# The attention stage of a hybrid layer: one written order on four engines, the sink logit as a column of the scores, output-projection rows split earlier

## The chip, the cores and the metric

The kernel runs on one core of a Trainium2 chip. The metric is device time in microseconds of that core. It holds all tensors in float32; matrix products that need accuracy are made from float32r halves (a high part and the rest), three matmuls for one product.

## The reference, cut to what matters

The layer is a diffusion backbone block: a modulated RMS norm, one input projection whose columns feed an mLSTM head group and a windowed attention head group, one output projection over both, a gated residual, and a convolutional GLU mixer. The change touches the attention group and the output projection that is woven into it.

```python
# q: (1024, 8, 64) rotated and scaled; k, v: (1024, 2, 64); k_ctx, v_ctx: (256, 2, 64); sink: (8,)
s_band = einsum(q, k)                # three blocks of 128 keys around each block of 128 queries,
s_band = where(|i - j| <= 128, s_band, -inf)
s_ctx  = einsum(q, k_ctx)            # 256 context keys, no mask
s_sink = sink[head]                  # one learned logit for each head
p   = softmax(concat([s_band, s_ctx, s_sink], -1), -1)
y_a = p[band] @ v + p[ctx] @ v_ctx   # the sink has no value row
x   = x + g_a * (concat([y_m, y_a], -1) @ w_out)      # rows 0-511 of w_out serve the mLSTM half y_m
```

## The kernel before

The program is written in a tile framework. Inside a `manual_schedule` block the named engines run their instructions in the order in which they are written; everywhere else a planner with a cost table chooses the order on each engine. TensorE is PE, VectorE DVE, ScalarE ACT, GpSimd POOL; SP issues nearly all DMAs.

**Query projections.** `qgen` runs 16 projections (`qproj`, 24 matmuls of 128x256 each), rotates each (three DVE operations, `rotate`), splits and transposes it (`qtrans`) and stores it to DRAM (`q_d`). The first ones run woven into the last mLSTM head; when that head is done, the tiles of the attention stage are allocated, and each later projection also starts one piece of `kprep` (keys of one block of 128 tokens) and one entry of `loads`: two pieces of the value tile `vv`, then row block 0 of the output projection. `load_wo` loads 128 rows of `w_out` (a 128x1024 tile `wor`), multiplies them by the gate row `rga`, copies them to float32r (ACT) and subtracts (DVE) for the rest. In this stretch PE alone has a written order.

**Attention.** There are 32 pairs of heads: 8 query blocks times 4 pairs. Class `Pair` holds the steps: `S(j)` scores of one head into a two-bank PSUM tile `sps` (256 context columns and 256 or 384 band columns, then one or two mask matmuls), `mxo(j)` the negated maximum (DVE, and a second DVE operation that takes the minimum with the negated sink `nsink`), `ex(j)` the exponential with its sum (ACT), `nrm` (the sink's own exponential, its addition to the sum, the reciprocal, and two multiplications on POOL), `tr(i)` transposes of probabilities, two key blocks of two heads at a time, `hi(i)` and `lo(i)` their float32r halves (ACT and DVE), `pv(i)` the products with values into the PSUM tile `u`, and `y1`, `y2` which add the halves and store into `yTa`. Score tiles are single: one for each head of a pair. The loop of lines 1180 to 1234 writes step t with scores of pair t, normalisation of pair t-1 and products of pair t-2.

**Output projection in between.** `wout_m(b)` is the mLSTM half of the output projection for token block b: four transposes of `ym`, a split, then eight groups of three 128x512 matmuls into the single PSUM tile `po` (four groups for each half of the 1024 columns), with an addition of x and a store to `x2_d`. `wout_f(0)` is the attention half of block 0. These are generators; `slot()` advances them by a rate between the steps of the loop. Row blocks 1 to 3 of `w_out` are loaded after the projections (line 1166), row blocks 4 to 7 in blocks 4 to 6 (`WBS`). None of this stage is inside `manual_schedule`: the planner orders it on all engines.

**After the loop** the pools close, and a stage with a written order (line 1387) makes the attention half for the other blocks (`wout_n`), norms them and prepares the mixer.

Of the kernel before, what the change touches and what calls it, by code (L numbers as in the profile page):

```python
# [17 lines left out]
P = 128  # L18
# [20 lines left out]
RATE3 = 0.37  # L39
QB = 3  # L40
# [16 lines left out]
AHEAD = 4  # L57

# [15 lines left out]
def build(tc, I, out, dbg=None):  # L74
# [11 lines left out]
    nsink = cp.tile([P, AH], F32, name="nsink")  # L86
# [38 lines left out]
    hps = [p1.enter_context(tc.tile_pool(name=f"hp{n}", bufs=1)) for n in range(2)]  # L125
# [222 lines left out]
    with tc.manual_schedule(engines={mybir.EngineType.PE, mybir.EngineType.DVE, mybir.EngineType.Activation,  # L348
# [93 lines left out]
        V.tensor_scalar(out=nsink[:], in0=rwc("sink"), scalar1=-1.0, scalar2=None, op0=ALU.mult)  # L442
# [405 lines left out]
    def qproj(i, b):  # L848
        px = pd.tile([P, 512], F32, name="px", tag="d")
        for kt in range(KT):  # L850
            mm3(px[:, :256], hsl(0, kt, NC + b), hsl(1, kt, NC + b), wq[i][0][:, kt, :256], wq[i][1][:, kt, :256],
                kt == 0, kt == KT - 1)
            if kt % 2:
                yield 0.64
        if i == 0:
            zs.append(pq.tile([P, 2, 2 * P], F32, name="z", tag="p_", bufs=PB, padded_shape=[P, 2, 320]))
        rotate(zs[b][:, i], px[:, :256], 4, b)

    def qtrans(i, b):
# [9 lines left out]
        QT = pq.tile([P, 4, P], F32R, name="QTo", tag="QTo", bufs=2)  # L869
# [3 lines left out]
    def load_wo(kt, eng, pool, tag=None):  # L873
        raw = wm.tile([P, D], F32, name="wor", tag="wor", bufs=2)
        nc.sync.dma_start(raw[:], I["w_out"][kt * P:(kt + 1) * P, :])
        eng.tensor_tensor(out=raw[:], in0=raw[:], in1=rga[:], op=ALU.mult)
        hi, lo = (w4(F32R, "wo4") if tag else pool.tile([P, D], F32R, name=f"wo{n}{kt}") for n in "hl")
        S.copy(hi[:], raw[:])
        V.tensor_tensor(out=lo[:], in0=raw[:], in1=hi[:].bitcast(F32), op=ALU.subtract)
        return hi, lo  # L880
# [16 lines left out]
    zs, wos, kgens, loads = [], [], [], []  # L897
# [45 lines left out]
    for h in range(H):  # L943
# [20 lines left out]
        with tc.manual_schedule(engines=order_):  # L964
# [24 lines left out]
            if nh is None:  # L989
# [10 lines left out]
                loads += [lambda: load_vv(0), lambda: load_vv(1), lambda: wos.append(load_wo(0, V, wm))]  # L1000
# [18 lines left out]
    lw = lastk.enter_context(tc.tile_pool(name="lw", bufs=6))  # L1019
    w4 = lambda dt, n: lw.tile([P, D], dt, name=n, tag="w4")  # L1020
# [3 lines left out]
    def wout_m(b):  # L1024
        pt = pT.tile([P, 512], F32, name="pt", tag="l")
        for j in range(4):
            T.transpose(pt[:, j * P:(j + 1) * P], ym[:, b, j * P:(j + 1) * P], ident[:])
        yield
        ph = t2.tile([P, 512], F32R, name="ymh", tag="ymh", bufs=1)
        pl_ = t2.tile([P, 512], F32R, name="yml", tag="yml", bufs=1)  # L1030
        S.copy(ph[:], pt[:])
        yield
        V.tensor_tensor(out=pl_[:], in0=pt[:], in1=ph[:].bitcast(F32), op=ALU.subtract)
        xb = x2t()
        nc.sync.dma_start(xb[:], I["x"][b * P:(b + 1) * P, :])
        yield
        for n in range(2):
            ns = slice(512 * n, 512 * n + 512)
            po = pO.tile([P, 512], F32, name="po", tag="o")
            for kt in range(4):  # L1040
                js = slice(kt * P, (kt + 1) * P)
                mm3(po[:], ph[:, js], pl_[:, js], wos[kt][0][:, ns], wos[kt][1][:, ns], kt == 0, kt == 3)
                yield
            V.tensor_tensor(out=xb[:, ns], in0=po[:], in1=xb[:, ns], op=ALU.add)
            if n == 1:
                nc.sync.dma_start(x2_d[b][:], xb[:])
            yield

    def wout_f(b):
        bs = slice(b * P, (b + 1) * P)  # L1050
        yh = t2.tile([P, 4, P], F32R, name="yh", tag="ymh", bufs=1)
        yl = t2.tile([P, 4, P], F32R, name="yl", tag="yml", bufs=1)
        xb = t3.tile([P, D], F32, name="x2", tag="x2")
        xs[b] = xb[:]
        nc.sync.dma_start(xb[:], x2_d[b][:])
        S.copy(yh[:], yTa[:, :, bs])
        yield
        V.tensor_tensor(out=yl[:], in0=yTa[:, :, bs], in1=yh[:].bitcast(F32), op=ALU.subtract)
        yield
        for n in range(2):  # L1060
            ns = slice(512 * n, 512 * n + 512)
            po = pO.tile([P, 512], F32, name="po", tag="o")
            for kt in range(4):
                mm3(po[:], yh[:, kt], yl[:, kt], wos[4 + kt][0][:, ns], wos[4 + kt][1][:, ns], kt == 0, kt == 3)
                yield
            V.tensor_tensor(out=xb[:, ns], in0=po[:], in1=xb[:, ns], op=ALU.add)
            if n == 1:
                nc.sync.dma_start(x2_d[b][:], xb[:])
            yield

    class Pair:
        def __init__(self, b, g, r):
# [7 lines left out]
            self.p, self.sv, self.pt, self.ph, self.pl = [None] * 2, [None] * 2, [None] * 3, [None] * 3, [None] * 3  # L1080

        def S(self, j):
# [3 lines left out]
            sps = pSs[j][0].tile([P, 1024], F32, name="sps", tag=pSs[j][1])  # L1086
# [10 lines left out]
            self.sv[j] = sps[:, 256:256 + self.nk]  # L1097

        def mxo(self, j):
            V.tensor_reduce(out=self.nm[:, j:j + 1], in_=self.sv[j], axis=AX.X, op=ALU.max, negate=True)  # L1100
            V.tensor_tensor(out=self.nm[:, j:j + 1], in0=self.nm[:, j:j + 1], in1=nsink[:, self.h0 + j:self.h0 + j + 1],
                             op=ALU.min)

        def ex(self, j):
            self.p[j] = pq.tile([P, 640], F32, name="p_", tag="p_", bufs=PB)
            S.activation(self.p[j][:, :self.nk], self.sv[j], AF.Exp, bias=self.nm[:, j:j + 1], scale=1.0,
                         accum_out=self.ss[:, j:j + 1])
# [57 lines left out]

    wos += [load_wo(k, V, lw, "w4") for k in range(1, 4)]
    w0 = wout_m(0)
    next(w0)
    for g in qpend:
        next(g, 0)  # L1170
    for _ in w0:
        pass
    pdk.close()
    pSs = [(pk, "pp"), (pa_.enter_context(tc.tile_pool(name="pS", bufs=1, space=PSUM, side="right")), "s")]
    pairs = [(b, g, r) for b in range(NL) for g in range(KVH) for r in range(2)]
    live = {}
    fill = [wout_m(b) for b in range(1, NL)] + [wout_f(b) for b in range(NA)]
    rate = (13 * 7 + 12 * NA) / (8.0 * (len(pairs) + 2))
    null = type("N", (), {"__getattr__": lambda s, n: (lambda *a: None)})()
    for t in range(len(pairs) + 2):  # L1180
        blk, sub = divmod(t, 4)
        if sub == 0 and blk < NL:
            if blk + 1 < NL:
                lq = load_q(blk + 1)
            for kt in range(4, 8):
                if WBS[kt - 4] == blk:
                    with tc.issue_after(lq):
                        wos.append(load_wo(kt, G, wop))

        def slot(k=1.0):  # L1190
            global_debt[0] += rate * k
            while fill and global_debt[0] >= 1.0:
                global_debt[0] -= 1.0
                try:
                    next(fill[0])
                except StopIteration:
                    fill.pop(0)
        if t == 0:
            global_debt = [0.0]
        if t < len(pairs):  # L1200
            live[t] = Pair(*pairs[t])
        A = live.get(t, null)
        B = live.get(t - 1, null)
        C = live.get(t - 2, null)
        B.nrm()
        A.S(0)
        slot()
# [12 lines left out]
        C.lo(1)  # L1220
        C.pv(0)
        slot()
        A.ex(1)
        C.tr(2)
        C.hi(2)
        slot()
        C.lo(2)
        C.pv(1)
        slot()
        C.pv(2)  # L1230
        C.y1()
        slot()
        C.y2()
        live.pop(t - 2, None)
    for f_ in fill:
        for _ in f_:
            pass
# [8 lines left out]
    rst2 = ExitStack()  # L1246
    eW = top.enter_context(tc.tile_pool(name="eW", bufs=1, side="right", reuse_waits="tile"))
# [28 lines left out]
    def ysplit_h(b, eng=G):  # L1276
        ys[b] = [t3.tile([P, 4, P], F32R, name=f"y{n}", tag=f"y{n}", bufs=3 if n == "h" else 2) for n in "hl"]
# [769 lines left out]
```

## Time and profile before

| | |
|---|---|
| median of 3 runs | 1298.04 us (1297.0 to 1298.63) |
| the profiled execution | 1300.43 us |
| its span from first to last instruction | 1298.6 us |
| mean granted TensorE clock | 0.991 |
| busy in the span | PE 1255.1 us, DVE 993.2, ACT 630.7, POOL 208.1 |
| last matmul of the query projections starts | 402.12 us |
| first transpose of the stage after attention | 608.91 us |

Times in rows are microseconds from the span's start; a row of a timeline gives start, duration, engine, line, operation, output<-inputs, form and count, and in brackets the idle time of that engine before it and what ended it. PE's durations contain the drain of its pipeline, so successive starts and not durations tell what a matmul costs; the same holds, less strongly, for DVE and ACT.

### The profile page before, as it was taken

How to read it: one execution, taken by the hardware profiler on the slowest of the kernel's cores; microseconds unless marked ns; L12 is line 12 of the kernel's file. 1: busy time of each engine (PE TensorE's matmuls, PEld its weight loads, DVE VectorE, ACT ScalarE, POOL GpSimd, SP SyncE). 2: the span in 40 equal slices, each digit the busy share in tenths (PEclk: the TensorE clock that was granted, in tenths of full speed). 3: DMA queues.
4: the chain of work that ended last, by engine and by line, in shares of the span. 5: the costliest groups of instructions: out<-in, count | busy, mean ns of one | idle time of the engine just before them, and what ended most of it. 6: DMA issues, size and time to landing. Idle time of an engine off the chain costs nothing.

```text
span 1298.6 us, 19413 instructions
## 1 busy us (share of the span) xinstructions
PE 1255.1 (97%) x7071; PEld 1069.9 (82%) x7071; DVE 993.2 (76%) x1809; ACT 630.7 (49%) x1271; POOL 208.1 (16%) x171
## 2 busy tenths in 40 slices
PE   6999999999898999999989999999999999999997
PEld 4899998989897787888768888888888888788886
DVE  5763777867786789896898777777777776877887
ACT  6632555464864567676654333333333333434435
POOL 1200000000001223332412122222212222001000
PEclk9999999999998999999989999999999999999999
DMA  9431544352253313202423223332222336974653
GB/s 362 173 118 40 145 136 132 119 165 76 83 180 129 131 50 114 98 33 68 161 81 112 100 97 105 117 111 105 98 89 106 105 106 242 340 285 161 204 196 136
DMA packets 90417, 175.63 MB, mean 135 GB/s; under 512 B 12938, under 2 KB 29522, under 8 KB 90322
## 3 DMA queue, kind: packets, MB, share of 16 engines
q1 hardware_dynamic: 90034, 173.61, 39.4%
q8 instruction: 56, 0.92, 0.3%
q10 hardware_dynamic: 288, 0.79, 0.2%
q14 instruction: 39, 0.32, 0.1%
HBM read 136.04 MB, written 38.33 MB: 134 GB/s over the span
## 4 chain that ended last, share of the span: by engine, by line
PE 79%; DVE 9%; ACT 4%; DMA 4%; issue 2%; POOL 1%; SPq 0%; ACTq 0%; DVEq 0%; POOLq 0%
PE pd L1890 14%; PE pc L1382 9%; PE pa L1382 9%; PE pp L582 6%; PE pb L1382 4%; PE pe L1382 4%; PE pd L1382 4%; PE u L1152 3%; PE pv L301 2%; PE pv L303 2%; PE pv L302 2%; PE px L303 2%; PE px L301 2%; PE px L302 2%; PE po L301 1%
## 5 line engine op out<-in xcount | busy, mean ns | idle before, releaser
L1484 ACT CAST wh<-Rb 128x1024 fp32r<-128x1024 f32 (+1 forms) x66 | 59.5, 903 | 144.4 <-PE pd L1382 81.4
L1890 PE MATMUL pd<-dh,al 128*128 128x512 f32 x296 | 115.4, 390 | 0.7 <-DVE al L1256 0.7
L1890 PE MATMUL pd<-dh,ah 128*128 128x512 f32 x296 | 115.3, 390 | 0.0
L1890 PE MATMUL pd<-dl,ah 128*128 128x512 f32 x296 | 115.1, 389 | 0.0
L1382 PE MATMUL pc<-hB,wh 128*128 128x512 f32 x344 | 106.5, 391 | 1.1 <-DVE av L1461 1.1
L1382 PE MATMUL pa<-hB,wh 128*128 128x512 f32 x336 | 103.6, 389 | 0.0
L1272 DVE TENSOR_TENSOR wl<-Rb,wh 128x1024 fp32r<-128x1024 f32 (+1 forms) x66 | 68.9, 1045 | 39.6 <-ACT wh L1484 39.1
L1592 POOL TENSOR_TENSOR tt<-vt,tt 128x512 f32<-128x512 f32 x22 | 29.5, 1341 | 320.4 <-ACT tt L1586 320.4
L582 PE MATMUL pp<-hl,wh 128*128 128x512 f32 x256 | 79.3, 405 | 0.0
L1382 PEld LDWEIGHTS pc<-hB,wh 128*128 128x128 f32 x344 | 64.8, 189 | 15.0 <-DVE av L1461 1.5
L301 PE MATMUL pv<-wh,hl 128*128 128x256 f32 x256 | 75.9, 296 | 0.0
L1382 PEld LDWEIGHTS pa<-hB,wh 128*128 128x128 f32 x336 | 63.0, 188 | 13.4 <-ACT sn L1556 0.4
L303 PE MATMUL pv<-wh,hl 128*128 128x256 f32 x256 | 72.3, 283 | 0.0
L302 PE MATMUL pv<-wl,hl 128*128 128x256 f32 x256 | 72.3, 282 | 0.0
L1382 PE MATMUL pc<-hB,wl 128*128 128x512 f32 x172 | 67.0, 389 | 0.0
L1890 PEld LDWEIGHTS pd<-dh,al 128*128 128x128 f32 x296 | 55.6, 188 | 13.1 <-DVE al L1256 1.6
L1382 PE MATMUL pa<-hB,wl 128*128 128x512 f32 x168 | 65.4, 389 | 0.0
L1890 PEld LDWEIGHTS pd<-dh,ah 128*128 128x128 f32 x296 | 55.6, 188 | 11.7 <-ACT ah L1255 0.4
L1890 PEld LDWEIGHTS pd<-dl,ah 128*128 128x128 f32 x296 | 55.6, 188 | 11.6
L1117 POOL TENSOR_SCALAR p__5051<-p__5051,ss 128x512 f32<-128x512 f32 x1 | 0.7, 687 | 353.9 <-DVE ss L1114 353.9
L1136 ACT CAST ph<-pt 128x512 fp32r<-128x512 f32 (+1 forms) x88 | 45.4, 526 | 21.8 <-PE pt L1129 21.2
L1382 PE MATMUL pe<-hB,wh 128*128 128x512 f32 x176 | 54.2, 389 | 0.0
(1075 smaller groups left out, 3810.0 us busy)
## 6 DMA issues: line engine op xcount, KB each, us to landing
w<-in_w_ada_dram SPq DMA_DIRECT2D x64, 256.0 KB, 2.7
br<-in_w_down_dram SPq DMA_DIRECT2D x25, 512.0 KB, 6.1
Ra<-in_w_up_dram SPq DMA_DIRECT2D x22, 512.0 KB, 3.5
Rb<-in_w_up_dram SPq DMA_DIRECT2D x22, 512.0 KB, 3.6
ar<-act_s SPq DMA_DIRECT2D x44, 256.0 KB, 3.3
act_a<-tt SPq DMA_DIRECT2D x33, 256.0 KB, 2.0
act_s<-tt SPq DMA_DIRECT2D x33, 256.0 KB, 2.0
wr<-in_w_h_dram SPq DMA_DIRECT2D x16, 512.0 KB, 4.6
```

The lines of the kernel that those rows point to most:

```text
L301: T.matmul(ps, st_hi, mv_hi, start=first, stop=False)
L302: T.matmul(ps, st_hi, mv_lo, start=False, stop=False)
L303: T.matmul(ps, st_lo, mv_hi, start=False, stop=last)
L582: T.matmul(pp[:, 512 * n:512 * n + 512], wkq[sw][:, kt, cs], hl[n][part][:, kt, :], start=kt == 0 and sw + part == 0, stop=kt == KT - 1 an ...
L1117: G.tensor_scalar(out=self.p[j][:, w], in0=self.p[j][:, w], scalar1=self.ss[:, j:j + 1], scalar2=1.0, op0=ALU.mult, op1=ALU.mult)
L1136: S.copy(self.ph[i][:, :w], self.pt[i][:, :w])
L1152: T.matmul(self.u[:], vv[:, c, self.g], part[i][:, kk * 2 * P:(kk + 1) * 2 * P], start=kb + m == 0, stop=kb == last and m == 1)
L1272: sub = lambda e, o, x, y: e.tensor_tensor(out=o, in0=x, in1=y, op=ALU.subtract)
L1382: T.matmul(ps[:], wt[sw][:, j, ks], hB[part][:, blk, kt, :], start=first and kt == 0 and sw + part == 0, stop=last and kt == 3 and sw == 1 ...
L1484: S.copy(wt[0][:], src)
L1592: G.tensor_tensor(out=self.tt[:, h2_], in0=self.vt[:], in1=self.tt[:, h2_], op=ALU.mult)
L1890: T.matmul(ps[:], ac[sa][:, js], w[sw], start=first and n == 0, stop=last and n == 2, skip_group_check=not fresh)
```

## The change

Four things change together.

1. **Written order.** The whole attention stage is put inside one `manual_schedule` for PE, DVE, ACT and POOL. Products lag one more step: step t writes the scores of pair t (A), normalisation of pair t-1 (B), transposes, splits and the first product of pair t-2 (C), and the remaining products and the output of pair t-3 (E).
2. **The output projection** becomes class `Wout` with separate steps, and a table `more[(step, slot)]` says which of them stands in which of four slots of a step. `Wout.tr` uses the PSUM tile `po` in place of one of the two transposition tiles.
3. **The sink** is copied by ACT into the PSUM column behind the last band column (`sk`, 128x1), so that the maximum and the exponential run over 641 (or 513) columns and need no correction. Three small DVE operations and one ACT exponential for each pair go, one DVE operation for each head among them; two ACT copies for each pair come.
4. **Rows of `w_out`.** Row blocks 0 to 3 are loaded, multiplied and split during the last 11 query projections (`WOS`), with blocks 1 to 3 placed in the tiles of `hl[0]`, which the first eight projections read last; their pool moves to the right side and stays until attention ends. Blocks 4 to 7 are handled in halves by `rows_step` from steps 4, 6, 12 and 14 on. The tiles of the next stage other than `x2` move from pool `t3` to a pool `t4` that opens after attention. The pool tag `QTo` gets three buffers in place of two.

```diff
+WOT = (4, 6, 12, 14)
+WOS = [(0,), (0,), (0, 1), (0,), (1, 2), (1,), (1, 2), (2, 3), (2, 3), (3,), (3,)]
...
-    def load_wo(kt, eng, pool, tag=None):
+    def load_wo(kt, room, eng, halves=False):
         raw = wm.tile([P, D], F32, name="wor", tag="wor", bufs=2)
...
+        dma = nc.sync.dma_start(raw[:], I["w_out"][kt * P:(kt + 1) * P, :])
+        yield
+        hi, lo = room()
+        wos.append((hi, lo))
+        for cs in (slice(0, 512), slice(512, D)) if halves else (slice(0, D),):
+            eng.tensor_tensor(out=raw[:, cs], in0=raw[:, cs], in1=rga[:, cs], op=ALU.mult)
+            yield
+            S.copy(hi[:, cs], raw[:, cs])
+            yield
+            V.tensor_tensor(out=lo[:, cs], in0=raw[:, cs], in1=hi[:, cs].bitcast(F32), op=ALU.subtract)
+            yield
...
+            for k in wosteps.pop(0) if wosteps else ():
+                if k >= len(wog):
+                    wog.append(load_wo(k, lambda k=k: wo_room(k), V))
+                next(wog[k], None)
...
+        def sk(self, j):
+            self.sps[j] = pSs[j][0].tile([P, 1024], F32, name="sps", tag=pSs[j][1])
+            e = 512 + self.nb * P
+            S.copy(self.sps[j][:, e:e + 1], sink[:, self.h0 + j:self.h0 + j + 1])
...
-            self.sv[j] = sps[:, 256:256 + self.nk]
+            self.sv[j] = sps[:, 256:257 + self.nk]
...
             V.tensor_reduce(out=self.nm[:, j:j + 1], in_=self.sv[j], axis=AX.X, op=ALU.max, negate=True)
-            V.tensor_tensor(out=self.nm[:, j:j + 1], in0=self.nm[:, j:j + 1], in1=nsink[:, self.h0 + j:self.h0 + j + 1],
-                             op=ALU.min)
...
         def nrm(self):
-            sk = t2.tile([P, 2], F32, name="sk", tag="sk", bufs=4)
-            V.tensor_tensor(out=sk[:], in0=self.nm[:], in1=nsink[:, self.h0:self.h0 + 2], op=ALU.subtract)
-            S.activation(sk[:], sk[:], AF.Exp)
-            V.tensor_tensor(out=self.ss[:], in0=self.ss[:], in1=sk[:], op=ALU.add)
             V.reciprocal(self.ss[:], self.ss[:])
...
+    def token(w, t):
+        more[t, 1] += [w.load, w.tr]
+        more[t, 2] += [w.hi]
+        more[t + 1, 3] += [w.lo]
+        tail_of(w, t)
+
+    def tail_of(w, t):
+        m = lambda n, k: lambda: w.mm(n, k)
+        more[t + 1, 1] += [m(0, 0)]
+        more[t + 1, 2] += [m(0, 1)]
+        more[t + 2, 0] += [m(0, 2)]
+        more[t + 2, 1] += [m(0, 3), lambda: w.add(0)]
+        more[t + 3, 0] += [m(1, 0)]
+        more[t + 3, 1] += [m(1, 1)]
+        more[t + 3, 2] += [m(1, 2), m(1, 3), lambda: w.add(1)]
...
+    for b in range(1, NL):
+        token(Wout(b, 0), 4 * b - 2)
+    n = len(pairs)
+    more[n - 4, 0] += [f0.load]
+    more[n - 3, 2] += [f0.hi, f0.lo]
+    tail_of(f0, n - 2)
...
+        N, A, B, C, E = (live.get(t + 1 - i, null) for i in range(5))
+        A.S(0)
+        E.lo(2)
         B.nrm()
...
+        fill(t, 3)
+        rows_step()
...
+        E.pv(1)
         C.tr(0)
+        E.pv(2)
+        A.mxo(0)
         C.hi(0)
...
+        E.y1()
+        A.ex(0)
+        N.sk(0)
         C.lo(0)
...
+        E.y2()
+        fill(t, 0)
...
         C.tr(1)
+        if t:
+            A.S(1)
         C.hi(1)
         A.mxo(1)
...
+        fill(t, 1)
+        C.tr(2)
         C.lo(1)
+        A.ex(1)
+        N.sk(1)
+        C.hi(2)
+        fill(t, 2)
         C.pv(0)
```

## Rows read from the trace of the kernel before

**Rows 1.** The page's first part: busy time, share of the span and instructions of PE.
```profile
PE 1255.1 (97%) x7071; PEld 1069.9 (82%) x7071; DVE 993.2 (76%) x1809; ACT 630.7 (49%) x1271; POOL 208.1 (16%) x171
```

**Rows 2.** Busy time of each engine by stretch: start and end, length, busy time and instructions of PE, of its weight loads (PEld), DVE, ACT and POOL, then the granted clock, the DMA share and GB/s. The stretches are the first 38 us of attention, its middle, attention as a whole, and the projections before it.
```profile
402.20:440.00 37.80, 33.43 (x190) 26.83 (x188) 26.72 (x61) 19.98 (x49) 6.42 (x8) 0.91 0.40 135
440.00:590.00 150.00, 143.67 (x975) 119.31 (x975) 133.90 (x334) 104.31 (x271) 51.11 (x58) 0.99 0.21 74
...
402.20:603.30 201.10, 190.19 (x1241) 156.62 (x1240) 170.10 (x418) 131.80 (x337) 60.25 (x70) 0.97 0.24 83
...
371.50:402.20 30.70, 30.70 (x272) 30.70 (x271) 23.59 (x53) 15.34 (x33) 0.00 (x0) 1.00 0.67 212
```

**Rows 3.** Timeline of PE where it runs without a gap: a group of three matmuls of the output projection, two products with values, the scores of one inner head, and transposes. Behind them, from the timeline of the stage's start, the first score matmuls of two heads of block 0 that follow each other.
```profile
482.24 0.39 PE L301 MATMUL po<-wo,ymh 128*128 128x512 f32 x1
...
482.94 0.28 PE L1152 MATMUL u<-ph,vv 128*128 128x256 f32 x1
483.05 0.28 PE L1152 MATMUL u<-pl__5938,vv 128*128 128x256 f32 x1
483.17 0.28 PE L1089 MATMUL sps<-kT,QT 128*128 128x256 f32 x1
...
483.89 0.28 PE L1129 MATMUL pt<-ident,p__5828 128*128 128x128 f32 x1
484.01 0.27 PE L1129 MATMUL pt<-ident,p__5849 128*128 128x128 f32 x1
...
412.26 0.28 PE L1089 MATMUL sps<-kT,QT 128*128 128x256 f32 x1
...
412.77 0.37 PE L1089 MATMUL sps<-kT,QT 128*128 128x256 f32 x1
```

**Rows 4.** Timeline of PE at the end of attention: a matmul of the output projection, and the first transpose of the next stage.
```profile
603.28 0.39 PE L303 MATMUL po<-woh,yl 128*128 128x512 f32 x1
...
608.91 1.09 PE L1323 MATMUL pt<-ident,hn 128*128 128x128 f32 x8
```

**Rows 5.** Groups of DVE instructions by line and form between 440 and 590 us: count, busy time, mean ns of one, idle time before them.
```profile
L1100 DVE TENSOR_REDUCE nm<-sps 128x1 f32<-128x640 f32 x45 | 36.7, 816 | 3.4 <-PE sps L1096 2.9
L1101 DVE TENSOR_TENSOR nm<-nm,nsink 128x1 f32<-128x1 f32 x53 | 13.5, 255 | 0.3
...
L1113 DVE TENSOR_TENSOR ss<-ss,sk 128x2 f32<-128x2 f32 x26 | 6.1, 235 | 2.9 <-ACT sk L1112 2.6
...
L1111 DVE TENSOR_TENSOR sk<-nm,nsink 128x2 f32<-128x2 f32 x26 | 4.0, 156 | 0.3
```

**Rows 6.** Timeline of all engines at the start of attention: the load of the last of the first four row blocks, its multiplication and its copy, and the matmul that waits for it.
```profile
406.78 0.33 SPq L875 DMA_DIRECT2D wor<-in_w_out_dram  x1
...
412.03 1.23 DVE L876 TENSOR_TENSOR wor<-wor,rga 128x1024 f32<-128x1024 f32 x1 [1.46 <-DMA wor<-in_w_out_dram]
...
413.29 1.04 ACT L878 CAST wo<-wor 128x1024 fp32r<-128x1024 f32 x1 [1.85 <-DVE wor L876]
...
414.39 0.49 PE L301 MATMUL po<-wo,ymh 128*128 128x512 f32 x1 [0.82 <-ACT wo L878]
```

**Rows 7.** Timeline of DVE at two places where it runs without a gap: the addition of x, half of `y2`, then a maximum and two `lo` of both widths.
```profile
449.51 0.69 DVE L1044 TENSOR_TENSOR x<-po,x 128x512 f32<-128x512 f32 x1
450.12 0.27 DVE L1163 TENSOR_TENSOR yTa<-u,ut 64x128 f32<-64x128 f32 x1
450.40 0.29 DVE L1164 TENSOR_TENSOR yTa<-u,ut 64x128 f32<-64x128 f32 x1
...
452.59 0.81 DVE L1100 TENSOR_REDUCE nm<-sps 128x1 f32<-128x640 f32 x1
453.32 0.67 DVE L1142 TENSOR_TENSOR pl__5513<-pt,ph 128x512 fp32r<-128x512 f32 x1
453.92 0.14 DVE L1101 TENSOR_TENSOR nm<-nm,nsink 128x1 f32<-128x1 f32 x1
453.99 0.41 DVE L1142 TENSOR_TENSOR pl__5531<-pt,ph 128x256 fp32r<-128x256 f32 x1
454.32 0.14 DVE L1111 TENSOR_TENSOR sk<-nm,nsink 128x2 f32<-128x2 f32 x1
```

**Rows 8.** The answers for lines 1101 and 1113 alone, between 402 and 606 us: count, and the shortest, middle and longest duration in ns.
```profile
L1101 DVE TENSOR_TENSOR nm<-nm,nsink x64: 138/153/1341, 406.7 to 592.0; 128x1 f32<-128x1 f32 x64
...
L1113 DVE TENSOR_TENSOR ss<-ss,sk x32: 142/160/2219, 413.2 to 593.7; 128x2 f32<-128x2 f32 x32
```

**Rows 9.** Timeline of ACT: half of `y1`, the sink's exponential, `hi`, the exponential of a head, and the next `hi`.
```profile
444.56 0.26 ACT L1158 COPY ut<-u 64x128 f32<-64x128 f32 x1
444.84 0.20 ACT L1112 ACTIVATE sk<-sk 128x2 f32<-128x2 f32 x1
444.95 0.57 ACT L1136 CAST ph<-pt 128x512 fp32r<-128x512 f32 x1
445.41 0.80 ACT L1106 ACTIVATE p__5423<-sps,nm 128x640 f32<-128x640 f32 x1
...
446.19 0.58 ACT L1136 CAST ph<-pt 128x512 fp32r<-128x512 f32 x1
```

**Rows 10.** Timeline of DVE in the last query projections: the first rotation of two of them.
```profile
395.80 0.42 DVE L313 TENSOR_TENSOR ta<-px,rope 128x256 f32<-128x256 f32 x1 [0.88 <-PE px L303]
...
399.20 0.42 DVE L313 TENSOR_TENSOR ta<-px,rope 128x256 f32<-128x256 f32 x1 [1.28 <-PE px L303]
```

More of the change, by code (lines that the diff above doesn't have):

```diff
@@ L441, in build @@
         V.tensor_copy(amask[:], amf)
-        V.tensor_scalar(out=nsink[:], in0=rwc("sink"), scalar1=-1.0, scalar2=None, op0=ALU.mult)
+        V.tensor_copy(sink[:], rwc("sink"))
         px_out(9)
@@ L1018, in build @@
     lastk = ExitStack()
-    lw = lastk.enter_context(tc.tile_pool(name="lw", bufs=6))
-    w4 = lambda dt, n: lw.tile([P, D], dt, name=n, tag="w4")
+    lw = lastk.enter_context(tc.tile_pool(name="lw", bufs=1))
     x2t = lambda: lw.tile([P, D], F32, name="x2", tag="x2", bufs=2)
     t2 = pa_.enter_context(tc.tile_pool(name="t2", bufs=2))
[L1024 to L1037, printed above, removed]
-            ns = slice(512 * n, 512 * n + 512)
[L1039 to L1044, printed above, removed]
-            if n == 1:
-                nc.sync.dma_start(x2_d[b][:], xb[:])
-            yield
@@ L1164, in y2 @@
             V.tensor_tensor(out=yf[64:128], in0=u[64:128, P:2 * P], in1=ut[64:128], op=ALU.add)
[L1166 to L1174, printed above, removed]
     pairs = [(b, g, r) for b in range(NL) for g in range(KVH) for r in range(2)]
+    pSs = [(pk, "pp")]
+    null = type("N", (), {"__getattr__": lambda s, n: (lambda *a: None)})()
@@ L1176, in build @@
     live = {}
[L1177 to L1180, printed above, removed]
-        blk, sub = divmod(t, 4)
[L1182 to L1197, printed above, removed]
-        if t == 0:
[L1199 to L1207, printed above, removed]
+    wogs = []
@@ new lines, in rows_step @@
+    def rows_step():
+        for q in list(wogs):
+            if next(q, 0) == 0:
+                wogs.remove(q)
+    more = collections.defaultdict(list)
+    def token(w, t):
[12 more added lines that the diff above has]
+        more[t + 3, 2] += [m(1, 2), m(1, 3), lambda: w.add(1)]
@@ new lines, in fill @@
+    def fill(t, i):
+        for f_ in more.pop((t, i), ()):
+            f_()
+    w0, f0 = Wout(0, 0), Wout(0, 1)
+    more[0, 0] = [lambda k=k: w0.mm(0, k) for k in range(4)] + [lambda: w0.add(0)]
+    more[0, 2] = [lambda k=k: w0.mm(1, k) for k in range(2)]
+    more[1, 0] = [lambda: w0.mm(1, 2)]
+    more[1, 1] = [lambda: w0.mm(1, 3), lambda: w0.add(1)]
+    for b in range(1, NL):
[3 more added lines that the diff above has]
+    more[n - 3, 2] += [f0.hi, f0.lo]
@@ new lines, in build @@
+    tail_of(f0, n - 2)
+    attn = tc.manual_schedule(engines={mybir.EngineType.PE, mybir.EngineType.DVE, mybir.EngineType.Activation,
+                                       mybir.EngineType.Pool})
+    attn.__enter__()
+    live[0] = Pair(*pairs[0])
+    live[0].sk(0)
+    w0.load()
+    for t in range(n + 2):
+        blk, sub = divmod(t, 4)
+        if sub == 0 and blk + 1 < NL:
+            lq = load_q(blk + 1)
+        if t in WOT:
+            k = 4 + WOT.index(t)
+            room = [wop.tile([P, D], F32R, name=f"wo{n}{k}")[:] for n in "hl"]
+            with tc.issue_after(lq):
+                wogs.append(load_wo(k, lambda room=room: room, G, True))
+                next(wogs[-1])
+        if t + 1 < len(pairs):
+            live[t + 1] = Pair(*pairs[t + 1])
+        N, A, B, C, E = (live.get(t + 1 - i, null) for i in range(5))
+        A.S(0)
+        E.lo(2)
+        B.nrm()
+        fill(t, 3)
+        rows_step()
+        if t == 0:
+            next(qpend.pop(0), 0)
+            w0.tr()
+            pdk.close()
+            pSs.append((pa_.enter_context(tc.tile_pool(name="pS", bufs=1, space=PSUM, side="right")), "s"))
+            live[0].sk(1)
+            w0.hi()
+            live[0].S(1)
+            w0.lo()
+        E.pv(1)
@@ L1221, in build @@
+        N.sk(1)
+        C.hi(2)
+        fill(t, 2)
         C.pv(0)
[L1222 to L1237, printed above, removed]
+        live.pop(t - 3, None)
+    E = live[n - 1]
+    E.lo(2)
+    E.pv(1)
+    E.pv(2)
+    E.y1()
+    E.y2()
+    for k in sorted(more):
+        fill(*k)
@@ L1238, in build @@
+    assert not wogs
+    attn.__exit__(None, None, None)
     pa_.close()
```

105 lines of the change are left out of this document (58 added, 47 removed).

## The prediction

> **What bounds the kernel now.** I read the page's first part, then busy time by stretch, then the dense places of each engine's timeline. The first part makes PE the engine of the kernel [rows 1], and by busy time attention looks full too: 190.2 of 201.1 us [rows 2]. That figure misleads, because a matmul's duration holds the drain of the pipeline. Where PE has no gap, a group of three 512-wide matmuls starts every 0.70 us (0.39 us is the length of each), two products of 256 take 0.23, the scores of an inner head 0.72, a transpose 0.11 to 0.12, the scores of a head of block 0 0.51 [rows 3]. So an inner pair costs PE 2 x 0.72 + 10 x 0.115 + 10 x 0.115 = 3.74 us, a pair of the first or last block 2 x 0.51 + 8 x 0.115 + 8 x 0.115 = 2.86, an output-projection block 8 x 0.70 + 4 x 0.115 = 6.06. Attention holds 24 inner and 8 outer pairs, eight blocks and eight groups of `wout_f(0)`: 89.8 + 22.9 + 48.5 + 5.6 = 166.8 us, with the last transposes of the projections about 168.3.
>
> Where does the stage end? The first transpose of the next stage starts at 608.91 [rows 4], and the 24 matmuls ahead of it take 8 x 0.70 = 5.6, so PE's attention work ends at 603.3, and the stage takes 201.1 us. PE lacks work for 201.1 - 168.3 = 32.8 us of it. That is the purse of this change.
>
> Skill and row differ on how large it is. The Trainium skill, Perfetto Trace Analysis, section Identifying the Most-Contended Engine, says that matmul busy time is a bad measure and that the busy share of weight loads is a better one. The trace agrees with the first half; by the second, 156.6 of 201.1 us of weight loads would leave 44 us, and the start spacing leaves 33. Nothing below uses it.
>
> **Why PE lacks work.** In the middle, 26 pairs pass in 150 us (26 additions of the sink's part, [rows 5]), 5.77 us each, where PE needs 3.74 + 6.06/4 = 5.26. DVE is busy 133.9 of these 150 us [rows 2], so it is the engine that PE waits for. In the first 38 us the granted clock is 0.91 [rows 2], between the levels of 1.2 and 2.4 GHz, and a load of `w_out` rows issued at 406.78 reaches DVE at 412.03, ACT at 413.29 and PE at 414.39 [rows 6]: there the stage waits for weights.
>
> **The sink (edit 3).** Removed for each pair on DVE: two minima of 255 ns, a subtraction of 156, an addition of 235 [rows 5], 0.90 us, 29 us in the stage. Their start spacing without neighbours is 0.07 to 0.08 [rows 5, 7]; the means are longer since some of them last to 1.34 and 2.22 us where the middle is 0.15 and 0.16 [rows 8]. The lower bound of what goes is thus 4 x 0.075 = 0.3 us a pair, the upper 0.9. The ACT exponential goes too (0.11 us between starts, [rows 9]), and two one-column ACT copies come. The trace has no ACT copy of one column; the nearest row is that exponential of two columns, so 0.11 us each (0 to 0.26, the 64x128 copy). One column more in maximum and exponential is 1/640 of 0.73 and 0.78 us: nothing.
>
> Those long tiny operations have two SBUF inputs, and the Trainium skill, SBUF — State Buffer, section SBUF: two separate sides, says that such a DVE operation and a GpSimd operation exclude each other for the whole instruction. The spread in [rows 8] fits that; by the rule the whole 0.90 us would be saved, by the spacing 0.3.
>
> **DVE and ACT in a step after the change.** DVE: `lo(2)` 0.33, reciprocal 0.1, two maxima 2 x 0.73, two `lo` 2 x 0.60, `y2` 0.28 + 0.30 (the estimate for its second half is its length) [rows 7]: 3.67; a quarter of a block's split and two additions, 3 x 0.61/4 = 0.46; the four remaining row blocks 4 x 1.2/32 = 0.15. Sum 4.3 us. ACT: exponentials 2 x 0.78, `hi` 2 x 0.46 and half that for the narrow one, `y1` 2 x 0.28, `sk` 0.22, and 0.3 for the rest [rows 9]: 3.8. Both lie under PE's 5.26. So if no chain between them is longer, PE sets the step.
>
> **The written order (edits 1 and 2).** The longest loop that I find: `lo(2)` on DVE heads the step, and behind it in DVE's queue stand the reciprocal, `mxo(0)`, `lo(0)`, `y2` and `mxo(1)`; that releases `ex(1)` on ACT, behind which stand `sk(1)` and `hi(2)`, which releases `lo(2)` of the next step. 0.33 + 0.1 + 0.73 + 0.60 + 0.58 + 0.81 = 3.15, block and row work on DVE in front of the second maximum 0.3, ACT 0.78 + 0.11 + 0.4 = 1.29, three hand-overs of about 0.05 (the copy of 413.29 starts 0.03 after the multiplication ends, [rows 6]): 4.9 us. That is below 5.26. The score tiles: `S` 0.72, maximum 0.8, exponential 0.8, `sk` 0.1, under 3 us. A step with four fill groups takes PE 6.5 us and one with only transposes of `ym` 4.2, so DVE and ACT get back in the long step what they lose in the short one. Following the queues by hand through such four steps gives waits of PE of 0.1 us in three places, about 0.08 us a step; a wait of `pv(1)` on `lo(1)` is the first to grow. I take 0.1 us x 28 steps = 2.8 us (bounds 0, and 0.45 x 28 = 12.6, if the steps only come to 5.7).
>
> **Start.** Row blocks 0 to 3 now are ready when the projections end, so the eight groups of block 0 and the first scores fill steps 0 and 1. What is left is the chain from `ym`'s transposes over `hi` and `lo` (0.6 + 0.6) and the first maximum: 3 us (1 to 6). **Drain:** the last steps have products and the eight groups of `Wout(0, 1)`, but small pairs whose loop of 4 us is longer than their 2.86: 3 us (2 to 5). **Hand-over:** the copy and subtraction that the next stage's first block needs now stand behind `y1` of the last pair on ACT, 2 x 0.28 + 0.5 + 0.6 [rows 7, 9], and perhaps behind a 1.04 us copy of mixer weights: 2.5 us (1 to 4). That covers the new pool `t4`; its tiles are first written there, when the tiles below have long been stored.
>
> **Row blocks moved (edit 4).** Into the last 31 us of projections come three casts of 1.04 on ACT, one multiplication and three subtractions of 1.2 on DVE (two multiplications and all of block 0 stand there already), 4.8 us beside 23.6 busy of 30.7 [rows 2]; DVE waits for PE there by 0.9 to 1.3 us in a projection [rows 10], which is the cover. Without it PE would stand for up to one such operation behind each rotation, 4 x 1.2. The four loads on SP pass the stores of `q_d` and the key loads; at a DMA share of 0.67 they may come late, but nobody needs block 3 before step 0. 2 us (0 to 5).
>
> **Sum.** 2.8 + 3 + 3 + 2.5 + 2 = 13.3 us of losses on 168.3: 181.6 in place of 201.1, a gain of 19.5. The profiled execution took 1300.43 (span 1298.6), so 1280.9; the median of the runs is 2.4 below the profiled execution, so **1278.5**. With all lower bounds (4 us) the gain is 28.8, time 1269; with all upper ones (32.6) nothing is gained. Taking one or two of them at their ends, the forecast's own range is 1271 to 1286.
>
> **Rivals.** *The loop of DVE and ACT binds* (0.18). Then a step takes 5.6 us instead of 5.36; if the hand-overs are nearer 0.25 us or the tiny copies 0.26, the loop comes to 5.6 to 5.7. 28 x 0.3 = 8 us more: 1287 (1284 to 1293). For it speaks that the queues now may not pass a waiting instruction: the Trainium skill, PSUM — Partial Sum Buffer, section Engine vs sequencer instructions, calls the other engines' queues strictly first in, first out and lets PE pull only weight loads ahead. The planner's order is such a queue too, so this alone gives no time. Against the rival: 0.36 us of slack.
> *The projections pay* (0.07). Bursts of 1.2 us on DVE and late loads hold the rotations: 5 us there and 3 more at the start: 1284 to 1288, if rows show PE waiting in `px`.
> *Given back behind the stage* (0.06). Attention ends early, but the next stage waits for the tiles of `t4` and for loads: within 0.2% of before. Against it: the next stage's first matmuls start in the old trace as soon as PE has finished this one [rows 4], and need nothing but its results.
> *Slower* (0.07). One mechanism: `E.lo(2)` at the head of DVE's step waits for `hi(2)`, the last of ACT's step, and `pv(1)` and the transposes of PE stand behind. It decides from a loop of 6.2 us a step, where 32 steps, start and drain together reach 201; at 6.6 us the kernel takes 13 us more, 1311. It needs 1.3 us more than my 4.9, say ACT's copy into PSUM at 0.7 us with a wait on the previous reader; nothing in [rows 9] is so slow.
>
> **How the numbers follow.** Forecast 0.62, rivals 0.18, 0.07, 0.06, 0.07. The range 1270 to 1293 holds the forecast but for its outer bounds, and the first two rivals, about 0.83. Faster by over 0.2% (2.6 us, about what a measurement of this kernel can tell from no change) 0.87, within 0.06, slower 0.07.
>
> **What would show it.** Steps of about 5.4 us between the maxima of inner pairs (before 5.77); the first 38 us with a granted clock of 0.95 or more and no wait for `wor`; no `nm` operation of one column; PE in the projections still without gaps; the first transposes of `hn` near 589. The forecast is wrong if the steps stay above 5.6, which then must show as `lo(2)` waiting for `hi(2)` or PE waiting for `lo`, or if PE stands before the next stage for more than 4 us.

## The result

| | before | after |
|---|---|---|
| median of the runs | 1297.68 us (1297.0 to 1298.63) | 1285.82 us (1285.7 to 1286.36) |
| profiled execution, its span | 1300.43, 1298.6 us | 1285.76, 1284.0 us |
| last projection matmul, first transpose of the next stage | 402.12, 608.91 us | 402.00, 593.00 us |

The ratio is 0.9906 (95% interval 0.9891 to 0.9922), a gain of 11.9 us. The forecast of 1278.5 had the sign. The time lies 7.3 us above it, and inside the forecast's own range of 1271 to 1286 by 0.2 us.

The page's line of busy time, and the stretches of the stage (the columns as in [rows 2]):

```profile
PE 1244.3 (97%) x7071; PEld 1064.4 (83%) x7071; DVE 972.5 (76%) x1685; ACT 638.6 (50%) x1307; POOL 210.1 (16%) x175
402.20:440.00 37.80, 35.94 (x248) 30.56 (x247) 26.74 (x53) 26.66 (x73) 11.76 (x15) 1.00 0.49 173
440.00:590.00 150.00, 145.45 (x1004) 123.85 (x1003) 118.90 (x239) 112.39 (x301) 50.79 (x60) 1.00 0.20 68
371.50:402.20 30.70, 30.53 (x265) 30.18 (x264) 26.60 (x56) 17.34 (x36) 0.00 (x0) 1.00 0.72 227
```

Against [rows 1, 2]: PE runs as many instructions. In the first 38 us it gets through 248 in place of 190, and the granted clock is 1.00 for 0.91; the only wait for a load of `wor` there is POOL's, 1.8 us for row block 4. DVE's middle is down from 133.9 to 118.9 us, ACT's up from 104.3 to 112.4. The projections carry 3 us more of DVE, and PE ends them at the same place (402.00 for 402.12). The end of the stage, PE's timeline (compare [rows 4]):

```profile
585.44 0.39 PE L1170 MATMUL u<-pl__7458,vv 128*128 128x256 f32 x2
587.14 0.50 PE L307 MATMUL po<-woh,yh 128*128 128x512 f32 x1 [1.31 <-ACT yh L1342]
...
592.76 0.39 PE L309 MATMUL po<-woh,yl 128*128 128x512 f32 x1
593.00 1.03 PE L1387 MATMUL pt<-ident,hn 128*128 128x128 f32 x8
```

**Steps.** The first score matmul of a pair marks a step. The starts of steps 14 to 18:

```profile
477.96 0.28 PE L1113 MATMUL sps<-kT,QT 128*128 128x256 f32 x1
...
482.34 0.28 PE L1113 MATMUL sps<-kT,QT 128*128 128x256 f32 x1
...
487.96 0.28 PE L1113 MATMUL sps<-kT,QT 128*128 128x256 f32 x1
...
493.28 0.28 PE L1113 MATMUL sps<-kT,QT 128*128 128x256 f32 x1
...
500.12 0.28 PE L1113 MATMUL sps<-kT,QT 128*128 128x256 f32 x1
```

A block has four kinds of steps: one with the transposes of `ym` only (4.38 us here), two with two groups of the projection (5.62, 5.32), one with four (6.84). Means over steps 6 to 27, read in the same way from each trace; PE's need is from the prediction's prices (pair 3.74, group 0.70, four transposes 0.46):

| us | ym transposes | first two groups | next two | four | block |
|---|---|---|---|---|---|
| PE's need | 4.20 | 5.14 | 5.14 | 6.54 | 21.02 |
| after | 4.38 | 5.93 | 5.32 | 6.74 | 22.37 |
| after, more DVE (e6) | 4.38 | 6.63 | 5.71 | 7.19 | 23.91 |
| after, no masks (e7) | 4.17 | 5.93 | 5.13 | 6.66 | 21.89 |
| after, old sink (e4) | 4.73 | 7.24 | 5.71 | 7.41 | 25.09 |

### The profile page after: what moved, and what is told of

Read it like the earlier page. It is cut to its first block, busy times and chain, and to the rows that moved or that the text cites. A ratio compares the mean times of both kernels' runs of the same rounds, so it can differ in the third digit from the quotient of the medians.

```text
span 1284.0 us, 19309 instructions
## 1 busy us (share of the span) xinstructions
PE 1244.3 (97%) x7071; PEld 1064.4 (83%) x7071; DVE 972.5 (76%) x1685; ACT 638.6 (50%) x1307; POOL 210.1 (16%) x175
## 4 chain that ended last, share of the span: by engine, by line
PE 82%; DVE 6%; ACT 5%; DMA 3%; issue 2%; POOL 1%; SPq 0%; DVEq 0%; ACTq 0%; POOLq 0%
PE pd L1954 14%; PE pa L1446 9%; PE pc L1446 8%; PE pp L588 6%; PE pb L1446 4%; PE pe L1446 4%; PE pd L1446 4%; PE u L1170 3%; PE po L307 2%; PE pv L307 2%; PE pv L309 2%; PE pv L308 2%; PE pt L1147 2%; PE po L309 2%; PE po L308 2%
```

## The experiments

After the result, my theory was: PE sets the steps after the change, at a floor a little higher than predicted because float32 transposes and float32r products alternate; the written order brought the gain. The rival: the loop of DVE and ACT sets them. Ratios are to the kernel before on the same chip, whose medians lay between 1297.7 and 1300.1 us, so ratios are compared and not times; 0.001 is 1.3 us.

| run | ratio, 95% interval |
|---|---|
| after | 0.9906 (0.9891 to 0.9922) |
| e1 before, sink only | 0.9956 (0.9943 to 0.9968) |
| e2 before, rows only | 0.9967 (0.9953 to 0.9982) |
| e5 before, sink and rows | 0.9925 (0.9913 to 0.9938) |
| e3 after, planner's order | 0.9881 (0.9866 to 0.9896) |
| e10 planner, products two behind | 0.9862 (0.9847 to 0.9877) |
| e11 e10 with the old buffers | 0.9898 (0.9881 to 0.9914) |
| e12 e10, row blocks and end retimed | 0.9887 (0.9869 to 0.9906) |
| e4 after, old sink | 1.0040 (1.0027 to 1.0052) |
| e6 after, more DVE | 0.9990 (0.9981 to 0.9999) |
| e7 after, no masks | 0.9871 (0.9856 to 0.9887) |
| e9 after, 3, 2 and 3 groups | 0.9938 (0.9926 to 0.9951) |

**e1, e2, e5: the sink and the rows on the kernel before.** e1, in `Pair.S` and below (e5 is e1 and e2 together):

```diff
+            S.copy(sps[:, 512 + nb * P:513 + nb * P], sink[:, h:h + 1])
-            self.sv[j] = sps[:, 256:256 + self.nk]
+            self.sv[j] = sps[:, 256:257 + self.nk]
...
-            V.tensor_tensor(out=self.nm[:, j:j + 1], in0=self.nm[:, j:j + 1], in1=nsink[:, self.h0 + j:self.h0 + j + 1],
-                             op=ALU.min)
```

> The kernel before with edit 3 alone: the sink as a column of the scores, everything else and the planner's order as before. Theory (the order of the work on the engines made PE wait, not the amount of DVE work): a step stays near 5.7 us and the time at 1294 to 1298. Rival (DVE's amount of work was the bound): 0.3 to 0.9 us of DVE work go from each of about 30 steps, so 9 us or more are gained until PE is full, 1281 to 1289.

e2, the first part of edit 4 (row blocks 0 to 3, with `WOS` and `wo_room` as in the changed kernel; blocks 4 to 7 stay as before):

```diff
-    wos += [load_wo(k, V, lw, "w4") for k in range(1, 4)]
+            for k in wosteps.pop(0) if wosteps else ():
```

> The kernel before with edit 4 alone: row blocks 0 to 3 of w_out are loaded and split during the last 11 query projections; planner's order, sink as before. Theory: the first 38 us, where PE's starts were 11.2 us longer apart than its dense spacing before and 2.9 to 5 us after, lose the wait for weights: 6 us gained, 1292 (1289 to 1294). Rival (the wait for rows only covers the chain of the first pair): within 2 us of before, 1296 to 1299.

> The kernel before with edits 3 and 4 together, products two steps behind, planner's order. If the two parts only add (ratios 0.9956 and 0.9967 alone), 0.992, 1288 to 1289 where before is at 1299; the rest of the gain then belongs to the written order, to the later products and to the steps of the output projection. Rival (the two free each other, and the rest is worth nothing): 0.988 to 0.989, as the changed kernel with the planner's order.

Alone the sink brings 0.0044 (5.7 us, 0.18 a pair) and the rows 0.0033 (4.3 us); together 0.0075, which is their sum. e1 lies between its two expectations: DVE was part of the bound, not all. e2's gain lies at the low end of the 4 to 9 us of its theory. The first 38 us of e2, then e1's middle:

```profile
402.20:440.00 37.80, 36.91 (x246) 30.75 (x245) 28.62 (x76) 22.79 (x59) 7.67 (x11) 1.00 0.45 151
```
```profile
440.00:590.00 150.00, 144.26 (x1008) 121.89 (x1007) 122.04 (x238) 108.74 (x302) 52.90 (x60) 1.00 0.21 71
```

With the early rows alone PE's first 38 us look as in the changed kernel, clock included. With the sink alone DVE falls to 122 us and PE gets 1008 matmuls into the middle, against 975.

**e3, e10: is it the order?** e3 takes the `manual_schedule` away; e10 also writes `lo(2)`, `pv(1)`, `pv(2)`, `y1`, `y2` of pair t-2 at the end of the step.

```diff
-    attn.__enter__()
...
         C.pv(0)
+        C.lo(2)
+        C.pv(1)
+        C.pv(2)
+        C.y1()
+        C.y2()
-        E.lo(2)
-        E.pv(1)
-        E.pv(2)
```

> The changed kernel without the written order of the attention stage: the planner orders the same instructions. Theory: the written order is what took most out of the steps, so the time goes back by 5 to 10 us, 1291 to 1296. Rival (sink and early rows carry the gain, and any order would do): 1285 to 1288.

> The changed kernel with the planner's order, and products and output written two steps behind the scores as before, in place of three. Before with sink and rows came to a ratio of 0.9925 and the changed kernel with the planner's order to 0.9881: 5.7 us of gain that are neither the sink nor the early rows nor the written order. Theory (the later products are what they come from): 0.9915 to 0.993. Rival (they come from the separate steps of the output projection, the split row blocks and the third buffer): 0.9875 to 0.989.

Both theories fall, that the written order brought the gain and that the later products did. The planner's order on the changed code is not slower but 0.0025 faster, with intervals that barely overlap (0.9891 to 0.9896). Its blocks take 22.35 us and its last scores start at 571.28, in the written order 22.37 and 571.34; what differs is the end, where the planner starts the last projection groups earlier and sets them singly between the pairs' matmuls; the next stage starts 2 us earlier. The other 1.2 us by which the span is shorter (1280.8 for 1284.0) lie behind that. The later products bring nothing either (22.07 us a block without them). First transposes of the next stage, in e3 and in e10:

```profile
590.99 1.03 PE L1383 MATMUL pt<-ident,hn 128*128 128x128 f32 x8
```
```profile
590.64 1.03 PE L1377 MATMUL pt<-ident,hn 128*128 128x128 f32 x8
```

**e11, e12: what is left.** From e5 to e10 lie 0.0063, 8 us, that are neither the sink nor the early rows, in the planner's order in both.

```diff
         def tr(self):
-            self.po = pO.tile([P, 512], F32, name="po", tag="o")
+            self.po = pT.tile([P, 512], F32, name="pt", tag="l")
...
-                self.pl[i] = pq.tile([P, 512], F32R, name="pl_", tag="QTo", bufs=3)
+                self.pl[i] = pq.tile([P, 512], F32R, name="pl_", tag="QTo", bufs=2)
```

> The run before (planner's order, products two behind) with two buffers for the float32r halves (tag QTo) in place of three, and the transposes of ym in one of the two transposition tiles as before, in place of the projection's tile. Open is where the 8 us between before with sink and rows (ratio 0.9925) and the run before (0.9862) come from. Theory (the buffers: a transposition tile or a half that comes free late holds PE): 0.990 to 0.993. Rival (the table of the output projection with its fixed places, and the split row blocks): 0.9855 to 0.9875.

The two buffers are 0.0036 of it (4.7 us); the rest, 3.5 us, lies in what else differs: the table of the projection, the halves of the row blocks, the order of the lines in a step, and sink copies a step ahead. No run separates these, and none separates the two buffers. PE's waits in e11 show the tile: between 440 and 563 us the transposes of `ym` wait for a `lo` five times, 2.2 us in all. Three of them:

```profile
PE pt L1057 <- DVE pl__6985 L1160: 0.5, 1, 0.5
PE pt L1057 <- DVE pl__6671 L1160: 0.5, 1, 0.5
PE pt L1057 <- DVE pl__6356 L1160: 0.5, 1, 0.5
```

e12 moves work of e10:

```diff
-WOT = (4, 6, 12, 14)
+WOT = (4, 8, 12, 16)
...
-    tail_of(f0, n - 2)
+    tail_of(f0, n - 3)
```

> The planner's order with products two behind (ratio 0.9862), row blocks 4 to 7 loaded from steps 4, 8, 12 and 16 on, and the attention half of block 0 one step earlier. Theory (what is left are the steps in which halves of the row blocks fall on DVE, 8 to 9 us long where others of their kind take 6 to 7, and 1 us at the end): 2 to 4 us faster, 0.983 to 0.985. Rival (the planner moves such work where it fits anyway): 0.9855 to 0.987.

It is no faster, rather slower, and misses both expectations; e10 stays the best version measured, 0.0044 ahead of the changed kernel. So the other parts bring 0.0138 in the planner's order, and the written order with products three steps behind gives back 0.0044 of it.

**e4: the old sink in the written order.** `mxo`, `ex` and `nrm` as before:

```diff
-            S.copy(self.sps[j][:, e:e + 1], sink[:, self.h0 + j:self.h0 + j + 1])
...
+            V.tensor_tensor(out=sk[:], in0=self.nm[:], in1=nsink[:, self.h0:self.h0 + 2], op=ALU.subtract)
+            S.activation(sk[:], sk[:], AF.Exp)
+            V.tensor_tensor(out=self.ss[:], in0=self.ss[:], in1=sk[:], op=ALU.add)
             V.reciprocal(self.ss[:], self.ss[:])
```

> The changed kernel with edit 3 undone: minimum with the negated sink, subtraction, exponential and addition as before, inside the written order; no column copies on ACT. Theory (PE sets the step after the change, with about 0.6 us of slack in the loop of DVE and ACT): 1286 to 1289. Rival (the loop of DVE and ACT sets the step): 0.3 to 0.9 us more in each of 30 steps, 1295 to 1312.

The result, 17.4 us above the changed kernel and above the kernel before, lies where the rival put it. DVE's groups between 440 and 563 us, then its timeline at one place:

```profile
L1135 DVE TENSOR_TENSOR ss<-ss,sk 128x2 f32<-128x2 f32 x20 | 3.2, 161 | 5.8 <-ACT sk L1134 5.8
```
```profile
487.00 0.15 DVE L1133 TENSOR_TENSOR sk<-nm,nsink 128x2 f32<-128x2 f32 x1
487.49 0.16 DVE L1135 TENSOR_TENSOR ss<-ss,sk 128x2 f32<-128x2 f32 x1 [0.34 <-ACT sk L1134]
487.68 0.17 DVE L1136 RECIPROCAL ss<-ss 128x2 f32<-128x2 f32 x1
487.76 0.69 DVE L891 TENSOR_TENSOR wol<-wor,woh 128x512 fp32r<-128x512 f32 x1
488.37 0.82 DVE L1122 TENSOR_REDUCE nm<-sps 128x1 f32<-128x640 f32 x1
```

DVE subtracts, waits for ACT's exponential, adds, and in the written order the maximum stands behind that: 5.8 us of waiting in 20 steps, 0.29 each, on top of the four operations. In the planner's order of before the same wait is 2.6 us for 26 [rows 5]. So the written order didn't bring the gain, but it needs the sink edit: worth 5.7 us under the planner, 17 inside this order.

**e6, e7: which engine sets a step?** One DVE operation more, and less PE work:

```diff
+            V.tensor_reduce(out=self.nmx[:, j:j + 1], in_=self.sv[j][:, 0:256], axis=AX.X, op=ALU.max, negate=True)
```

> The changed kernel with one DVE operation more behind each maximum: a second maximum over the 256 context columns, into a scratch column that nobody reads, some 0.35 us, 0.7 us in a step. Theory (PE sets the step, and the loop of DVE and ACT has 0.2 to 0.6 us of slack): 3 to 15 us slower than the changed kernel, 1289 to 1301. Rival (the loop sets the step): all of 30 x 0.7, 21 us slower, 1306 or more. If DVE had slack enough: within 3 us, 1285 to 1289.

```diff
-            if b > 0:
-                T.matmul(band[:, 0:P], identb[:], amask[:, 0], start=False, stop=b == NL - 1)
-            if b < NL - 1:
-                T.matmul(band[:, (nb - 1) * P:nb * P], identb[:], amask[:, 1], start=False, stop=True)
```

> The changed kernel without the 112 mask matmuls of the scores (band edges then count as allowed keys); nothing on DVE, ACT or POOL changes. A mask costs PE 0.06 us between starts. Theory (PE sets the step): 5 to 9 us faster than the changed kernel, 1277 to 1281. Rival (the loop of DVE and ACT sets the step): within 2 us of the changed kernel, 1284 to 1287.

10.9 us slower, inside the range of the theory, and 4.5 us faster, between the two expectations: PE sets some steps and not others. The table of steps says which. The extra operations (two a step, mean 415 ns) add 0.70 us to the first step with two groups and nothing to the step before it; the missing masks (4 x 0.055 us in a step, by e8) take 0.21 from that step and nothing from the other. The `ym` step is PE's, the next one belongs to the loop of DVE and ACT, and the other two answer to both. It is the loop and not the amount of DVE's work: in steps 7 and 15 of the changed kernel DVE is busy 4.8 of 5.6 us, less than PE's need of 5.14, and stands 0.62 us waiting for ACT's `hi(2)`. DVE at the head of step 19, with that wait, and PE's wait in the same step:

```profile
506.12 0.42 DVE L1160 TENSOR_TENSOR pl__6408<-pt,ph 128x256 fp32r<-128x256 f32 x1 [0.63 <-ACT ph L1154]
506.46 0.16 DVE L1132 RECIPROCAL ss<-ss 128x2 f32<-128x2 f32 x1
506.61 0.69 DVE L1074 TENSOR_TENSOR yml<-po,ymh 128x512 fp32r<-128x512 f32 x1
507.22 0.93 DVE L891 TENSOR_TENSOR wol<-wor,woh 128x512 fp32r<-128x512 f32 x1
508.07 0.81 DVE L1124 TENSOR_REDUCE nm<-sps 128x1 f32<-128x641 f32 x1
508.81 0.68 DVE L1160 TENSOR_TENSOR pl__6436<-pt,ph 128x512 fp32r<-128x512 f32 x1
```
```profile
509.54 0.33 PE L1147 MATMUL pt<-ident,p__6268 128*128 128x128 f32 x1 [0.65 <-DVE pl__6436 L1160]
```

The split of `ym`'s rest, and in steps 11 and 19 half a row block, stand ahead of the first maximum; `lo(0)`, behind it, frees the transposition tile that `tr(2)` needs. Steps 11 and 19 take 6.46 and 6.47 us, steps 7 and 15 without the half block 5.63 and 5.62.

**e8: what does a change of matmul kind cost?** Extra work on PE that nobody reads:

```diff
+    ptr = lambda n: [T.transpose(ppt[:, i % 4 * P:i % 4 * P + P], ym[:, i % 8, 0:P], ident[:]) for i in range(n)]
+    pmm = lambda n: [T.matmul(ppo[:, 0:256], QTs[NL - 1][:, i % 8], kT2[0][:, 0, 0:256], start=True, stop=True) for i in range(n)]
...
+    for i in range(16):
+        ptr(4)
+        pmm(2)
+    ptr(64)
+    pmm(32)
```

> The changed kernel with extra work for PE at the end of attention that nobody reads: 16 times four transposes and two products of 256 columns in turn, then 64 transposes and 32 products in two runs; the same with two mask matmuls for the transposes, and with masks and transposes. Theory (each change between float32 transposes and float32r products costs PE 0.05 to 0.1 us): the alternating order takes 1.5 to 3 us longer than the two runs for its 31 changes. Rival (the wider spacing seen at a change is only how the record models starts): both orders take the same time within 0.3 us.

The alternating order began at 586.49; the start of the two runs, and the same for masks with products and masks with transposes:

```profile
597.28 7.15 PE L1302 MATMUL ppt<-ident,ym 128*128 128x128 f32 x64
604.18 4.07 PE L1303 MATMUL ppo<-kT,QT 128*128 128x256 f32 x32
608.09 0.28 PE L1304 MATMUL ppo<-amask,identb 128*128 128x128 bf16 x2
...
614.81 1.96 PE L1304 MATMUL ppo<-amask,identb 128*128 128x128 bf16 x32
616.58 4.07 PE L1303 MATMUL ppo<-kT,QT 128*128 128x256 f32 x32
620.49 0.28 PE L1304 MATMUL ppo<-amask,identb 128*128 128x128 bf16 x2
...
629.38 1.95 PE L1304 MATMUL ppo<-amask,identb 128*128 128x128 bf16 x32
631.17 7.16 PE L1302 MATMUL ppt<-ident,ym 128*128 128x128 f32 x64
638.08 0.48 PE L307 MATMUL po<-woh,yh 128*128 128x512 f32 x1
```

Transposes and products: 597.28 - 586.49 = 10.79 us in turn, 608.09 - 597.28 = 10.81 in two runs. The theory falls: in this one execution that change is free, and the wider spacing behind transposes belongs to the record. Masks and products: 6.72 against 5.68, 0.03 us for each of 31 changes; masks and transposes: 8.89 against 8.70.

**e9: the same instructions at other places.** Three, two and three groups, row blocks at steps 4, 8, 12, 16, the last groups spread over the end.

```diff
-WOT = (4, 6, 12, 14)
+WOT = (4, 8, 12, 16)
...
+        more[t + 1, 0] += [m(0, 0)]
+        more[t + 1, 1] += [m(0, 1)]
+        more[t + 1, 2] += [m(0, 2)]
+        more[t + 2, 0] += [m(0, 3), lambda: w.add(0)]
+        more[t + 2, 2] += [m(1, 0)]
+        more[t + 3, 0] += [m(1, 1)]
```

> The changed kernel with another table, the same instructions. The groups of the output projection stand 3, 2 and 3 in the three steps behind the ym transposes in place of 2, 2 and 4; the second halves of row blocks 4 to 7 fall due in steps where DVE has time (loads at 4, 8, 12, 16); the groups of the attention half of block 0 begin one step earlier, and the last of them stands behind the last products with values. Theory (after the change some steps are set by PE and others by the loop of DVE and ACT, and what one step leaves idle the next can't use): steps behind the ym transposes from 5.9 to about 6.0 us with one group more, the four-group step from 6.7 to 6.0 to 6.1, 2 to 3 us less in the middle; 1.6 us from the row blocks; 1.5 to 2 us from the drain; together 4 to 7 us faster than the changed kernel, ratio 0.985 to 0.9875 against before. Rival (PE is full apart from 0.3 us a step that no order removes): within 2 us of the changed kernel, ratio 0.989 to 0.992.

4 us slower than the changed kernel, against both expectations. The steps come to 4.37, 7.02, 5.73 and 5.92 us: the last is PE's (need 5.84), but the first step with groups, 1.2 above its need of 5.84, now has a group in its first slot that waits for the split of `ym`, and the next waits for the addition that empties `po`:

```profile
489.65 0.47 PE L307 MATMUL po<-woh,ymh 128*128 128x512 f32 x1 [0.46 <-DVE yml L1074]
...
498.17 0.50 PE L307 MATMUL po<-woh,ymh 128*128 128x512 f32 x1 [0.30 <-DVE x L1085]
```

One part of its theory holds: with the half blocks moved, steps 11 and 19 are as long as the others of their kind (7.00, 7.01 against 6.99, 7.00).

## Why the prediction was right, and where it was not

- **Purse and bound.** Right: PE lacked work at the start and in the steps, and filling both is the gain; DVE's fall in the middle agrees.
- **Steps**, the term that was mis-sized. Predicted 0.1 us over 5.26 in each of 28 steps, 2.8 us; measured 22.37 us a block for a need of 21.02, 0.34 a step, 9.4 us in 28. What failed is the sentence that DVE and ACT get back in the long step what they lose in the short one. The prediction added up the loop of DVE and ACT once, with an average of 0.3 us of block and row work in it, and held 4.9 against PE's average of 5.26. But a step costs the larger of PE's need and the loop in that step. The split of `ym` falls into one kind of step, 0.6 us, and in steps 11 and 19 half a row block with it, 1.5 us together. With them the predicted loop comes to 5.2 and 6.1 us where PE needs 5.14; measured were 5.62 and 6.46, so 0.4 us of the loop is in none of its terms. This kind of step takes 0.79 us over PE's need on average (e6 and e7 show that it is not PE's). The other three kinds lie 0.18 to 0.20 above PE's need. The masks are not the cause of that: without them (e7) the `ym` step takes 4.17 us, still 0.19 over a need that is then 3.98. The cause stays open.
- **The first rival** (the loop of DVE and ACT binds, 5.6 us a step, 1284 to 1293) came nearer than the forecast: 5.59 us a step in the mean of a block, and 1285.8. Its mechanism is half right, for one kind of step in full, for two in part, for the `ym` step not. The sign that the prediction named for it is there, `lo(2)` waiting 0.63 us for `hi(2)` (506.12), and the lock was also `lo(0)`, which frees the tile for `tr(2)`.
- **The sink.** 0.3 to 0.9 us a pair by its rows; under the planner 0.18, below the lower bound; inside the written order 0.54 (17.4 us over 32 pairs), because there the round trip to ACT counts too. The prediction gave that round trip no price. The long tiny operations are shown, though: in the trace of before all 18 operations of lines 1101, 1111 and 1113 that last over 250 ns overlap a POOL operation and end within 20 ns behind its end; of the 110 shorter ones 105 overlap none. The longest:

```profile
525.95 2.37 POOL L876 TENSOR_TENSOR wor<-wor,rga 128x1024 f32<-128x1024 f32 x1 [3.79 <-DMA wor<-in_w_out_dram]
526.12 2.22 DVE L1113 TENSOR_TENSOR ss<-ss,sk 128x2 f32<-128x2 f32 x1
```

- **The written order.** I read edits 1 and 2 as the cure of the steps and never priced the same code under the planner. e3 shows that the order carries none of the gain; e11 that the two buffers, which I passed over, carry 4.7 us under the planner.
- **Start, drain, hand-over, projections.** By PE's starts beyond its dense spacing, the start costs 2.9 us (predicted 3) and the drain 3.2 (3). The hand-over is 1.31 us and a short wait for `yl`, about 1.5 (2.5), and the projections nothing (2). The cover named for them held.
- **The sum.** The stage took 587.4 - 402.1 = 185.3 us for 181.6. The floor of 168.3 and the terms as measured, 9.4, 2.9, 3.2 and 1.5, give 185.3, so the floor held. The steps cost 6.6 us more than predicted, the hand-over and the projections 3.0 less: without that luck the time would have left the forecast's own range. The next stage started 15.9 us earlier and the program ended 14.6 earlier. What lies behind the stage took 691.0 us for 689.7; in the other runs, e8 left aside, it takes between 689.4 and 691.4 without following one edit, so this 1.3 stays open. And the 2.4 us from profiled execution to median were a property of that one execution of before: the one of after lies on its median. 3.7 + 1.3 + 2.4 = 7.4 of the 7.3.

## What to carry to other kernels

In a written order a step costs the larger of two things in that step: the need of the engine that should be full, and the loop through the others, waits included. Add up both for every kind of step, with the work that comes once a block, before averaging. Price a written order against the planner on the same changed code, and a removed operation by the round trip between engines that it closes, not by its length alone. A buffer more, or a tile that borrows another pool's, may be worth as much as the order.

## What the hardware showed that was not expected

Alternating float32 transposes with float32r products cost PE nothing (10.79 against 10.81 us), while bf16 masks between products cost 0.03 us a change. An ACT copy of one column into PSUM takes 163 ns, always (162 to 165, 63 times). Its price in the step is less: the next `hi` starts about 0.10 us behind it, so that the 0.11 between starts that the prediction took from another operation was about right:

```profile
L1104 ACT COPY sps<-sink x63: 162/163/165, 404.6 to 572.3; 128x1 f32<-128x1 f32 x63
```
```profile
504.10 0.16 ACT L1104 COPY sps<-sink 128x1 f32<-128x1 f32 x1
504.19 0.58 ACT L1154 CAST ph<-pt 128x512 fp32r<-128x512 f32 x1
```
